# A decoder layer on one Trainium2 core: rows of x in own places and a chunk ahead, gated rows' transposes a chunk later, four chunks of seven products in the second gate/up unit

## The chip, the cores and the metric

The kernel runs on one core of one Trainium2 chip. The metric is the device time of one execution in microseconds. Three executions of the kernel before gave 2029.17, 2032.1 and 2034.15 us, median 2032.1 us. One more execution was recorded by the hardware profiler; it took 2031.15 us.

## What is computed

One layer of a decoder on 256 tokens of width 2048, in float32:

```python
h = h + 0.5 * swiglu(rmsnorm(h, g_ffn1[l]), w1_gate[l], w1_up[l], w1_down[l])
z = rmsnorm(h, g_mix[l]) @ w_in[l]
y = jnp.concatenate([rmsnorm(y_a, g_a_out[l]), rmsnorm(y_b, g_b_out[l])], axis=-1)
h = h + y @ w_out[l]
h = h + cross_attention(rmsnorm(h, g_x[l]), rmsnorm(mem, g_mem[l]),
                        w_xq[l], w_xkv[l], w_xo[l])
h = h + 0.5 * swiglu(rmsnorm(h, g_ffn2[l]), w2_gate[l], w2_up[l], w2_down[l])
```

The change concerns the two feed-forward blocks, `swiglu(x) = (silu(x @ w_gate) * (x @ w_up)) @ w_down`, with 2048 inputs and 5632 inner columns.

## The kernel before, in words

**Exactness.** TensorE is fed float32r values. Every float32 operand is split into a high part and a rest (`split`, L146: ScalarE casts the high part, VectorE subtracts it), and a product is made of three matmuls: high times high, rest times high, high times rest (`passes`, L424, and `run`, L444, whose matmul is L447).

**Units and chunks.** A feed-forward block begins with eleven gate/up units (`gu_unit`, L725). Unit `c` takes 512 columns of the gate and 512 of the up weights through all 2048 inputs, in eight chunks of 256 inputs. A chunk's weights are one load of 1 MB on SyncE's DMA queue (SP) into one of three `raw` places (`load`, L347), and are split into `wh` (ScalarE) and `wl` (VectorE), two places each. A chunk multiplies 2 by 2 blocks of tokens and inputs with 2 by 2 blocks of weights. Kind N does so by eight block products, 24 matmuls. Kind C also by eight, but arranged so that its results can be summed with those of kind S. Kind S does it by seven products (Strassen's way), 21 matmuls; for these VectorE also makes sums of weights (`t`, L356 to L360), which are split too (`th` on ScalarE, `tl` on VectorE). Of the other operand, the normed tokens, an S or C chunk needs differences of blocks as well as the blocks (`fill_sums`, L272, for the first block's `n1`). A pair of 128-row tiles of x, transposed, is called pair `i`; chunk `i` multiplies it. Pair 0 is of kind D, which holds the differences for both C and S.

**Which kinds.** `FEWER = "CCSCSCSC"` has three S chunks, `MORE = "SCSCSCSC"` four. In `gu_unit` (L737) units 2 to 9 take `MORE`, the others `FEWER`; in the first block, unit 0 is all N (`plain_gu_unit`, L753), since its tokens are still being split while it runs.

**Order of work.** TensorE's order is the program's. On the other engines a scheduler sets the order, at build time; it is fixed when the kernel runs. `push` (L513) first loads and splits a chunk's weights, then runs the chunk before it (`turn`, L505). `later` is a list of steps that are put off by a number of chunks. When a unit ends, `late` (L728) gathers its results (`seven_late`, L601), gates them (`gated`, L713), and `rows_done` (L692) puts off, for each of the two blocks of 128 tokens, `turned_rows` (L150): ScalarE copies the gated rows into two 16-bit halves (L153), and SP starts a DMA transpose of them (L156). The first block of tokens is put off by 0, the second by 1. SP issues in order: a weight load behind a transpose isn't issued before it.

**First unit of the first block.** `prep1` (L920) loads pair `i+1` of x while chunk `i` is prepared, into a place of a pool of six (`s2`), and, at 3 to 5, loads x itself and squares it for the norm. `first_pairs` (L889) scales pair `i` by the norm's gain, splits it in time for chunk `i`, and puts its differences off by one chunk.

Of the kernel before, what the change touches and what calls it, by code (L numbers as in the profile page):

```python
# [11 lines left out]
AF = mybir.ActivationFunctionType  # L12
ALU = mybir.AluOpType
# [4 lines left out]
TB = 2  # L18
# [15 lines left out]
def layer_kernel(  # L34
# [22 lines left out]
    nc = tc.nc  # L57
# [13 lines left out]
    def nm(s):  # L71
        uid[0] += 1
        return f"{s}_{uid[0]}"

    def m4(s):
        return mid.tile([P, 1024], F32, tag="m4", name=nm(s))

    def s2(s):
        return tmp.tile([P, 512], F32, tag="s2", name=nm(s))
# [4 lines left out]
    sm = const.tile([P, N_SMALL], F32, name="sm")  # L84
# [61 lines left out]
    def split(hi, lo, src):  # L146
        nc.scalar.copy(hi, src)  # L147
        nc.vector.tensor_tensor(lo, src, hi.bitcast(F32), ALU.subtract)  # L148

    def turned_rows(s, dst, src):  # L150

        w = s2(s + "w").bitcast(U16)
        nc.scalar.copy(  # L153
            w.rearrange("p (h c) -> p h c", h=2), src.bitcast(U16).rearrange("p (c h) -> p h c", h=2)
        )
        nc.sync.dma_start_transpose(dst, w)  # L156

    def tile_turned(s):
        return m4(s).bitcast(U16).rearrange("p (b c t) -> p b c t", b=TB, c=8)
# [109 lines left out]
            fill(s, p, raw)  # L269
        return p  # L270

    def fill_sums(s, p, raw):  # L272

        f = s2(s + "f").rearrange("p (k t) -> p k t", k=4)
        if p.kind == "C":
            f = f[:, :2, :]
            nc.vector.tensor_tensor(f, raw[:, 0::2, :], raw[:, 1::2, :], ALU.subtract)
        else:
            nc.vector.tensor_tensor(
                f[:, 0:2, :], raw[:, 1:2, :].to_broadcast([P, 2, P]), raw[:, 0::3, :], ALU.subtract  # L280
            )
            nc.vector.tensor_tensor(f[:, 2, :], raw[:, 0, :], f[:, 1, :], ALU.subtract)
            nc.vector.tensor_tensor(f[:, 3, :], raw[:, 2, :], f[:, 2, :], ALU.subtract)
        split(p.sums[0], p.sums[1], f)
        if p.kind == "D":
            d = s2(s + "d")[:, :256].rearrange("p (k t) -> p k t", k=2)
            nc.vector.tensor_tensor(d, raw[:, 0::2, :], raw[:, 1::2, :], ALU.subtract)
            split(p.more[0], p.more[1], d)

    def rows_of(srcT, i):  # L290
        return srcT[i * T:(i + 1) * T, :].rearrange("(k p) t -> p k t", p=P)
# [179 lines left out]
    piece = [0]  # L471
# [23 lines left out]
    later = []  # L495
# [17 lines left out]
    def push(u, i, w, p, post=None, pieces=None, beside=None, before=None, ending=None):  # L513
        if before is not None and i:
            before(i)
        b = load(u.s, w, u.kinds[i], pieces, lambda n: before(i, n) if i == 0 else None)
        if beside is not None:
            beside(i)

        def run():  # L520
            first, last = [f("S") if "S" in u.kinds else -1 for f in (u.kinds.find, u.kinds.rfind)]
            if u.late and all(name in u.left for name in u.late):
                held[0] = first <= i <= last

                ends[0] = now[0] + 2 if u.clear and i == first - 1 else None
            held[0] = held[0] or i in u.alone
            tight[0] = u.sparse and first <= i <= last
            if ending is None:
                u.multiply(u.kinds[i], p(), b, i in (0, len(u.kinds) - 1))
            elif not u.kept:  # L530
                u.kept.append((p(), b))
            else:
                u.multiply_two(u.kept[0], (p(), b), ending)
            held[0] = False
            ends[0] = None

        turn(run, post)
# [42 lines left out]
    FEWER, MORE = "CCSCSCSC", "SCSCSCSC"  # L580
# [20 lines left out]
    def seven_late(u, got, dst):  # L601

        p1, v, z = got["p1"], got["v"], got["z"]
        nc.vector.tensor_tensor(dst(0, 0), u["P2"], p1, ALU.add)
        nc.vector.tensor_tensor(dst(1, 1), u["Q5"], z, ALU.add)
        nc.vector.tensor_tensor(v, u["Q5"], v, ALU.add)  # L606
        nc.vector.tensor_tensor(dst(0, 1), u["Q3"], v, ALU.add)
        nc.vector.tensor_tensor(dst(1, 0), u["Q4"], z, ALU.subtract)
# [79 lines left out]
    def ffn(s, get, rs, wgu, wd, on_block, first=None, on_token_block=None):  # L688
# [3 lines left out]
        def rows_done(c, rows_):  # L692
            t = tile_turned(s + "a")

            def turned(tb):
                turned_rows(s, t[:, tb], rows_[tb])
                for q in range(2):
                    acts[2 * c + q] = t

            for tb in range(TB):  # L700
                later.append((tb, lambda tb=tb: turned(tb)))

        def joined(i):
            turned_ = by_block(have(acts, i))
# [8 lines left out]
        def gated(up, sg, r, tb):  # L713
            nc.scalar.activation(sg[1], sg[0], AF.Silu, scale=r[:, tb:tb + 1])
            nc.vector.scalar_tensor_tensor(
                out=sg[1], in0=up, scalar=r[:, tb:tb + 1], in1=sg[1], op0=ALU.mult, op1=ALU.mult
            )

        def inner(i):
            if pairs[i] is None:  # L720
                raw = joined(i)
                pairs[i] = Pair(s + "a", KINDS_D[i])
                fill(s + "a", pairs[i], raw)

        def gu_unit(c):  # L725
            got = {}

            def late(u):  # L728
                r = rs()
                c22 = s2(s + "u")  # L730
                at = {(0, 0): got["p1"], (1, 1): c22, (0, 1): got["v"], (1, 0): got["z"]}
                seven_late(u, got, lambda tb, j: at[tb, j])
                gated(at[0, 1], (at[0, 0], at[0, 0]), r, 0)
                gated(c22, (at[1, 0], at[1, 0]), r, 1)
                rows_done(c, (at[0, 0], at[1, 0]))

            kinds = MORE if 2 <= c <= 9 else FEWER  # L737
            order = range(8)
            if c == (first is not None):
                order = ORDER[first is None]  # L740
            u = Unit(s + "g", "".join(kinds[j] for j in order))
            for i in range(8):
                push(
                    u, i, wgu[order[i], c], lambda j=order[i]: get(j),
                    lambda i=i: (
                        i == u.kinds.rindex("S") and seven_early(u, got), i == 7 and late(u)
                    ),
                    beside=lambda i: (
                        rs() if (c, i) == (0, 5) else inner(i - 5) if c == 10 and i >= 5 else None
                    ),  # L750
                )
# [30 lines left out]
        for n, idx in enumerate(turns):  # L782
            half = n % 2
            kinds = "".join(KINDS_D[i] for i in idx)
# [98 lines left out]
    n1 = [None] * 8  # L883
    parts1 = tiny.tile([P, TB, NG], F32, tag="parts", name=nm("parts"))
    rs1 = []

    ahead = []

    def first_pairs(i, piece=None):  # L889

        if not piece:
            n1[i] = Pair("n1", KINDS[i], "N")
            if piece is not None:
                ahead.append(s2("n1r").rearrange("p (k t) -> p k t", k=2))
        if piece is None:
            for k in range(2):
                scaled_row(i, k)
            split(*[t.rearrange("p k t -> p (k t)") for t in n1[i].base],
                  ahead[0].rearrange("p k t -> p (k t)"))
        elif piece in (0, 2):  # L900
            k = piece // 2
            nc.sync.dma_start(ahead[0][:, k, :], xT[k * P:(k + 1) * P, :])
            row_loaded(n1[i], ahead[0], i, k, G_FFN1)
        if piece in (None, 2):
            raw = ahead.pop(0)

            def sums():
                if piece is not None:
                    for k in range(2):
                        scaled_row(i, k, raw)  # L910
                fill_sums("n1", n1[i], raw.rearrange("p k (b t) -> p (k b) t", b=TB))

            later.append((1, sums))

    def scaled_row(i, k, raw=None):
        o = (raw or ahead[0])[:, k, :]
        c = G_FFN1 + 2 * i + k
        nc.scalar.activation(o, o, AF.Copy, scale=sm[:, c:c + 1])

    def prep1(i):  # L920
        if i < 7:
            ahead.append(s2("n1r").rearrange("p (k t) -> p k t", k=2))
            nc.sync.dma_start(ahead[-1], rows_of(xT, i + 1))
        for j in {3:(0,1),4:(2,3)}.get(i, ()):
            blocks_of_x(j)
        for j in {4:(0,1),5:(2,3)}.get(i, ()):
            for tb in range(TB):
                square_into(parts1[:, tb, j:j + 1], h[:, tb, j * 512:(j + 1) * 512], 512)
        if i == 5:
            rs1.append(rstd_of(parts1, NG, D))  # L930

    def blocks_of_x(j0):
# [8 lines left out]
        first=(first_pairs, prep1),  # L941
# [573 lines left out]
```

## Time and profile before

| what | value |
|---|---|
| median of three executions | 2032.1 us |
| profiled execution, its own time | 2031.15 us |
| span of its profile, first to last instruction | 2029.3 us |
| TensorE busy | 2012.1 us, 99% |
| VectorE busy | 1854.5 us, 91% |
| ScalarE busy | 1306.9 us, 64% |
| granted TensorE clock, mean | 0.999 |
| HBM read | 398.52 MB, 197 GB/s over the span |

In the rows of the profile PE is TensorE's matmuls and PEld its weight loads, DVE is VectorE, ACT is ScalarE, POOL is GpSimd, SPq is SyncE's queue that issues DMAs. A row of the timeline has start in us, duration in us, engine, line, operation, out<-in, how often, and in brackets the idle time before it and what ended that. A row of the table of waits has the waiting engine and what it waited for, then us in total, times, and the longest. A row of a stretch has its bounds, its length, and for each engine busy us and (x) its number of instructions. In the view of one tile, an operation's duration is min/median/max in ns, and the time from issue to landing in us. A tile's name begins with the block's part: `f1g` is the first block's gate/up, `f1d` its down projection, `f2` the second block; `f1gQ`, `f1gP`, `f1gR` are accumulators, `f1gw` the loaded weights.

### The profile page before, as it was taken

To read this page: it belongs to the slowest core of one execution; us is meant where nothing else is said; L and a number is where in the kernel's file an instruction comes from. 1 tells how busy PE (TensorE), PEld (TensorE's weight loads), DVE (VectorE), ACT (ScalarE), POOL (GpSimd) and SP (SyncE) were. 2 spreads that over 40 slices of the span, in tenths; PEclk is the share of its full clock that TensorE was granted. 3 is DMA by queue.
4 is the path that set the end of the run, shared out by engine and by line. 5 is a ranking of instruction groups with operands and counts; after the bars stand their busy time and mean duration, and the time that the engine had idled before them with its cause. 6 is when DMAs were issued, how large, how long until landed. Compare 5 with 4: busy or idle time off the path is not lost.

```text
span 2029.3 us, 24175 instructions
## 1 busy us (share of the span) xinstructions
PE 2012.1 (99%) x9168; PEld 1664.4 (82%) x9168; DVE 1854.5 (91%) x1988; ACT 1306.9 (64%) x1440; POOL 34.0 (2%) x57
## 2 busy tenths in 40 slices
PE   9999999999999999999999999999999999999998
PEld 7888878888888888888888888888888888888886
DVE  6999999999999978989878977899999999999998
ACT  7656656567665766655557666675656665676664
POOL 0000000000000010100000000000000000000000
PEclk9999999999999999999999999999999999999999
DMA  8566666666555565545665544556666656665563
GB/s 312 201 240 206 214 218 200 228 216 220 203 192 206 184 240 191 192 166 175 210 218 188 205 149 148 181 186 228 198 235 213 219 204 238 209 218 206 187 227 125
DMA packets 115332, 415.82 MB, mean 205 GB/s; under 512 B 61824, under 2 KB 63888, under 8 KB 68112
## 3 DMA queue, kind: packets, MB, share of 16 engines
q1 hardware_dynamic: 112768, 407.14, 57.9%
q0 software_dynamic: 2016, 6.30, 1.0%
q8 instruction: 72, 1.18, 0.2%
q10 hardware_dynamic: 432, 0.84, 0.1%
q14 instruction: 44, 0.36, 0.1%
HBM read 398.52 MB, written 2.10 MB: 197 GB/s over the span
## 4 chain that ended last, share of the span: by engine, by line
PE 84%; DVE 7%; issue 4%; ACT 2%; DMA 2%; SPq 0%; POOL 0%; DVEq 0%; POOLq 0%; ACTq 0%
PE f2gQ L447 13%; PE f1gQ L447 11%; PE f2dQ L447 6%; PE f1dQ L447 6%; PE f2gP L447 4%; PE f1gP L447 4%; PE xqQ L447 3%; PE f2dP L447 3%; PE f1dP L447 3%; PE woQ L447 2%; PE xoQ L447 2%; PE f2dR L447 2%; PE f1dR L447 2%; PE mv0Q L447 2%; PE vQ L447 2%
## 5 line engine op out<-in xcount | busy, mean ns | idle before, releaser
L148 DVE TENSOR_TENSOR f1gwl<-f1gw,f1gwh 128x1536 fp32r<-128x1536 f32 (+2 forms) x94 | 181.6, 1934 | 23.2 <-ACT f1gwh L147 23.2
L147 ACT CAST f1gwh<-f1gw 128x1536 fp32r<-128x1536 f32 (+2 forms) x94 | 152.3, 1626 | 62.7 <-PE f1gQ L447 41.6
L147 ACT CAST f2gwh<-f2gw 128x1536 fp32r<-128x1536 f32 (+1 forms) x88 | 150.5, 1711 | 61.4 <-PE f2gQ L447 41.4
L148 DVE TENSOR_TENSOR f2gwl<-f2gw,f2gwh 128x1536 fp32r<-128x1536 f32 (+1 forms) x88 | 179.0, 2035 | 9.1 <-ACT f2gwh L147 9.1
L147 ACT CAST f2gth<-f2gt 128x1024 fp32r<-128x1024 f32 x82 | 85.8, 1050 | 67.5 <-DVE f2gt L360 37.8
L447 PE MATMUL f1gQ<-f1gwh,n1fh 128*128 128x512 f32 x318 | 124.3, 391 | 1.6 <-DVE f1gv L606 1.6
L447 PE MATMUL f2gQ<-f2gwh,n4fh 128*128 128x512 f32 x317 | 124.2, 392 | 0.3
L447 PE MATMUL f1gQ<-f1gwh,n1fl 128*128 128x512 f32 x318 | 123.7, 389 | 0.0
L447 PE MATMUL f2gQ<-f2gwh,n4fl 128*128 128x512 f32 x317 | 123.4, 389 | 0.0
L147 ACT CAST f1gth<-f1gt 128x1024 fp32r<-128x1024 f32 x76 | 79.4, 1051 | 63.7 <-DVE f1gt L360 38.2
L147 ACT CAST f2dwh<-f2dw 128x2048 fp32r<-128x2048 f32 (+1 forms) x44 | 77.4, 1760 | 47.4 <-PE f2dQ L447 42.6
L147 ACT CAST f1dwh<-f1dw 128x2048 fp32r<-128x2048 f32 (+1 forms) x44 | 77.3, 1757 | 40.9 <-PE f1dQ L447 37.2
L148 DVE TENSOR_TENSOR f1dwl<-f1dw,f1dwh 128x2048 fp32r<-128x2048 f32 (+1 forms) x44 | 92.1, 2092 | 11.5 <-ACT f1dwh L147 11.4
L148 DVE TENSOR_TENSOR f2dwl<-f2dw,f2dwh 128x2048 fp32r<-128x2048 f32 (+1 forms) x44 | 92.1, 2093 | 11.2 <-ACT f2dwh L147 11.1
L148 DVE TENSOR_TENSOR f2gtl<-f2gt,f2gth 128x1024 fp32r<-128x1024 f32 x82 | 99.6, 1217 | 1.0
L447 PE MATMUL f1gQ<-f1gwl,n1fh 128*128 128x512 f32 x318 | 97.5, 389 | 0.0
L447 PE MATMUL f2gQ<-f2gwl,n4fh 128*128 128x512 f32 x317 | 96.7, 389 | 0.0
L148 DVE TENSOR_TENSOR f1gtl<-f1gt,f1gth 128x1024 fp32r<-128x1024 f32 x76 | 92.2, 1218 | 1.0
L447 PEld LDWEIGHTS f1gQ<-f1gwh,n1fh 128*128 128x128 f32 x318 | 59.7, 188 | 15.8 <-DVE f1gv L606 3.5
L447 PEld LDWEIGHTS f2gQ<-f2gwh,n4fh 128*128 128x128 f32 x317 | 59.5, 188 | 14.8 <-DVE f2gv L606 2.6
L447 PE MATMUL f1gP<-f1gwh,n1fl 128*128 128x512 f32 x176 | 68.9, 392 | 1.3 <-DVE n1fl L148 1.3
L447 PEld LDWEIGHTS f1gQ<-f1gwl,n1fh 128*128 128x128 f32 x318 | 59.7, 188 | 12.6 <-DVE f1gwl L148 0.2
(790 smaller groups left out, 6017.5 us busy)
## 6 DMA issues: line engine op xcount, KB each, us to landing
f2gw<-in_w_gu SPq DMA_DIRECT2D x88, 1024.0 KB, 4.9
f1gw<-in_w_gu SPq DMA_DIRECT2D x86, 1024.0 KB, 5.2
f1dw<-in_w_down SPq DMA_DIRECT2D x44, 1024.0 KB, 4.8
f2dw<-in_w_down SPq DMA_DIRECT2D x44, 1024.0 KB, 4.8
wow<-in_w_out SPq DMA_DIRECT2D x16, 1024.0 KB, 4.9
xqw<-in_w_xq SPq DMA_DIRECT2D x16, 1024.0 KB, 4.8
xow<-in_w_xo SPq DMA_DIRECT2D x16, 1024.0 KB, 4.8
qw<-in_w_in SPq DMA_DIRECT2D x8, 1024.0 KB, 4.8
```

The source lines that it names most:

```text
L147: nc.scalar.copy(hi, src)
L148: nc.vector.tensor_tensor(lo, src, hi.bitcast(F32), ALU.subtract)
L447: nc.tensor.matmul(self.banks[name], x, y, start=name not in self.begun, stop=self.left[name] == 0)
```

## The change

Three things, in the first feed-forward block for the first two, in both blocks for the third:

- Pair `i` of x is loaded into a place of its own (halves of four tiles of the larger pool `m4`), loaded a chunk earlier for pairs 4 to 7, and split a chunk earlier: at chunk 3 pairs 3 and 4 are split, at chunks 4 to 6 pairs 5 to 7. Differences of pairs are put off by two chunks, those of pairs 2 and 3 by one. The loads and squares of x come a chunk later. For pairs 0 to 2 some of these instructions keep the program's order.
- In the first block, unit 1 takes `MORE` instead of `FEWER`: its chunk 0 is S instead of C.
- Transposes of gated rows are put off by 1 and 2 chunks instead of 0 and 1.

```diff
-                later.append((tb, lambda tb=tb: turned(tb)))
+                later.append((tb + 1, lambda tb=tb: turned(tb)))
...
-            kinds = MORE if 2 <= c <= 9 else FEWER
+            kinds = MORE if (2 if first is None else 1) <= c <= 9 else FEWER
...
+    def raw_x(i):
+
+        if i % 2 == 0:
+            raws.append(m4("n1r").rearrange("p (i k t) -> p i k t", i=2, k=2))
+        return raws[-1][:, i % 2]
 
     def first_pairs(i, piece=None):
+
+        if piece is not None or i < 3:
+            first_pair(i, piece)
+        elif i == 3:
+            first_pair(3)
+            first_pair(4)
+        elif i < 7:
+            first_pair(i + 1)
...
+                placed = tc.keep_in_program_order if i < 3 else lambda ins: ins
                 if piece is not None:
                     for k in range(2):
-                        scaled_row(i, k, raw)
-                fill_sums("n1", n1[i], raw.rearrange("p k (b t) -> p (k b) t", b=TB))
-
-            later.append((1, sums))
+                        placed(scaled_row(i, k, raw))
+                fill_sums("n1", n1[i], raw.rearrange("p k (b t) -> p (k b) t", b=TB), placed)
+
+            later.append((1 if i in (2, 3) else 2, sums))
...
     def prep1(i):
-        if i < 7:
-            ahead.append(s2("n1r").rearrange("p (k t) -> p k t", k=2))
-            nc.sync.dma_start(ahead[-1], rows_of(xT, i + 1))
-        for j in {3:(0,1),4:(2,3)}.get(i, ()):
+        for q in {0: (1,), 1: (2,), 2: (3, 4), 3: (5,), 4: (6,), 5: (7,)}.get(i, ()):
+            ahead.append(raw_x(q))
+            nc.sync.dma_start(ahead[-1], rows_of(xT, q))
+        for j in {4:(0,1),5:(2,3)}.get(i, ()):
             blocks_of_x(j)
-        for j in {4:(0,1),5:(2,3)}.get(i, ()):
+        for j in {5:(0,1),6:(2,3)}.get(i, ()):
             for tb in range(TB):
                 square_into(parts1[:, tb, j:j + 1], h[:, tb, j * 512:(j + 1) * 512], 512)
-        if i == 5:
+        if i == 6:
             rs1.append(rstd_of(parts1, NG, D))
```

**SP, at the end of the first block's unit 1** (`f1gw` are loads of weights for the following chunks, `f1a` the transposed gated rows of unit 1). Before:

```order
L377 DMA f1gw_936<-in_w_gu 128x2048
L156 DMA_TRANSPOSE f1a_853<-f1w_854 128x8x128
L156 DMA_TRANSPOSE f1a_853<-f1w_891 128x8x128
L354 DMA f1gw_963<-in_w_gu 128x2048
L377 DMA f1gw_1005<-in_w_gu 128x2048
```

Changed:

```order
L377 DMA f1gw_941<-in_w_gu 128x2048
L156 DMA_TRANSPOSE f1a_858<-f1w_893 128x8x128
L354 DMA f1gw_968<-in_w_gu 128x2048
L156 DMA_TRANSPOSE f1a_858<-f1w_938 128x8x128
L377 DMA f1gw_1010<-in_w_gu 128x2048
```

The first transpose stands where it stood; the second has moved behind one load of weights. It is so after units 0 to 8 of the first block and 1 to 8 of the second. After unit 10 of both, where one load stood between the two transposes, both now stand behind it; after the other units nothing moves on SP.

**ACT, in the first unit, from the cast of chunk 2's weights on.** Before, `f1gw_222` and `f1gw_264` are the weights of chunks 2 and 3, and `n1r_228` and `n1r_270` the rows of pairs 3 and 4:

```order
L147 CAST f1gwh_223<-f1gw_222 128x2048
L918 ACTIVATE n1r_228<-n1r_228,sm 128x256 x2
L147 CAST n1fh_258<-n1r_228 128x512
L147 CAST f1gwh_265<-f1gw_264 128x2048
L147 CAST n1fh_216<-n1f_298 128x512
```

Changed, `f1gw_209` and `f1gw_268` are those weights, and `n1r_128`, `n1r_171`, `n1r_216` hold pairs 0 and 1, 2 and 3, 4 and 5:

```order
L147 CAST f1gwh_210<-f1gw_209 128x2048
L936 ACTIVATE n1r_128<-n1r_128,sm 128x256 x2
L936 ACTIVATE n1r_171<-n1r_171,sm 128x256 x2
L936 ACTIVATE n1r_216<-n1r_216,sm 128x256 x2
L147 CAST f1gwh_269<-f1gw_268 128x2048
L147 CAST n1fh_124<-n1f_244 128x512
L147 CAST n1fh_254<-n1r_171 128x512
L147 CAST n1fh_260<-n1r_216 128x512
```

Six scalings of rows stand between the two casts of weights, and the casts of pairs 3 (`n1fh_254`) and 4 stand behind them.

**DVE, in the same place.** Before, `n1fl_259` is the rest of pair 3:

```order
L148 TENSOR_TENSOR f1gwl_224<-f1gw_222,f1gwh_223 128x2048
L148 TENSOR_TENSOR n1fl_259<-n1r_228,n1fh_258 128x512
L279 TENSOR_TENSOR n1f_298<-n1r_172 128x256
L282 TENSOR_TENSOR n1f_298<-n1r_172,n1f_298 128x128
L283 TENSOR_TENSOR n1f_298<-n1r_172,n1f_298 128x128
L148 TENSOR_TENSOR f1gwl_266<-f1gw_264,f1gwh_265 128x2048
```

Changed, `n1fl_255` is the rest of pair 3:

```order
L148 TENSOR_TENSOR f1gwl_211<-f1gw_209,f1gwh_210 128x2048
L279 TENSOR_TENSOR n1f_244<-n1r_128 128x256
L282 TENSOR_TENSOR n1f_244<-n1r_128,n1f_244 128x128
L283 TENSOR_TENSOR n1f_244<-n1r_128,n1f_244 128x128
L148 TENSOR_TENSOR f1gwl_270<-f1gw_268,f1gwh_269 128x2048
L148 TENSOR_TENSOR n1fl_125<-n1f_244,n1fh_124 128x512
L287 TENSOR_TENSOR n1d_250<-n1r_128 128x256
L148 TENSOR_TENSOR n1fl_255<-n1r_171,n1fh_254 128x512
```

The rest of pair 3 stood right behind the rest of chunk 2's weights; it now stands behind the rest of chunk 3's weights and the differences of pair 0.

More of the change, by code (lines that the diff above doesn't have):

```diff
@@ L270, in pair_from_rows, with fill_sums @@
         return p
-    def fill_sums(s, p, raw):
+    def fill_sums(s, p, raw, placed):
         f = s2(s + "f").rearrange("p (k t) -> p k t", k=4)
@@ L276, in fill_sums @@
             f = f[:, :2, :]
-            nc.vector.tensor_tensor(f, raw[:, 0::2, :], raw[:, 1::2, :], ALU.subtract)
+            placed(nc.vector.tensor_tensor(f, raw[:, 0::2, :], raw[:, 1::2, :], ALU.subtract))
         else:
-            nc.vector.tensor_tensor(
+            placed(nc.vector.tensor_tensor(
                 f[:, 0:2, :], raw[:, 1:2, :].to_broadcast([P, 2, P]), raw[:, 0::3, :], ALU.subtract
-            )
+            ))
             nc.vector.tensor_tensor(f[:, 2, :], raw[:, 0, :], f[:, 1, :], ALU.subtract)
@@ L286, in fill_sums @@
             d = s2(s + "d")[:, :256].rearrange("p (k t) -> p k t", k=2)
-            nc.vector.tensor_tensor(d, raw[:, 0::2, :], raw[:, 1::2, :], ALU.subtract)
+            placed(nc.vector.tensor_tensor(d, raw[:, 0::2, :], raw[:, 1::2, :], ALU.subtract))
             split(p.more[0], p.more[1], d)
@@ L887, in layer_kernel, with first_pair @@
     ahead = []
-    def first_pairs(i, piece=None):
+    raws = []
+    def raw_x(i):
+        if i % 2 == 0:
+            raws.append(m4("n1r").rearrange("p (i k t) -> p i k t", i=2, k=2))
+        return raws[-1][:, i % 2]
+    def first_pairs(i, piece=None):
+        if piece is not None or i < 3:
[5 more added lines that the diff above has]
+            first_pair(i + 1)
+    def first_pair(i, piece=None):
         if not piece:
@@ L893, in first_pairs @@
             if piece is not None:
-                ahead.append(s2("n1r").rearrange("p (k t) -> p k t", k=2))
+                ahead.append(raw_x(0))
         if piece is None:
@@ L917, in scaled_row @@
         c = G_FFN1 + 2 * i + k
-        nc.scalar.activation(o, o, AF.Copy, scale=sm[:, c:c + 1])
+        return nc.scalar.activation(o, o, AF.Copy, scale=sm[:, c:c + 1])
     def prep1(i):
-        if i < 7:
-            ahead.append(s2("n1r").rearrange("p (k t) -> p k t", k=2))
-            nc.sync.dma_start(ahead[-1], rows_of(xT, i + 1))
-        for j in {3:(0,1),4:(2,3)}.get(i, ()):
+        for q in {0: (1,), 1: (2,), 2: (3, 4), 3: (5,), 4: (6,), 5: (7,)}.get(i, ()):
+            ahead.append(raw_x(q))
+            nc.sync.dma_start(ahead[-1], rows_of(xT, q))
+        for j in {4:(0,1),5:(2,3)}.get(i, ()):
             blocks_of_x(j)
-        for j in {4:(0,1),5:(2,3)}.get(i, ()):
+        for j in {5:(0,1),6:(2,3)}.get(i, ()):
             for tb in range(TB):
                 square_into(parts1[:, tb, j:j + 1], h[:, tb, j * 512:(j + 1) * 512], 512)
-        if i == 5:
+        if i == 6:
             rs1.append(rstd_of(parts1, NG, D))
```

## The prediction

> **What bounds the kernel now.** First the page's busy times and its chain of waits:
>
> ```profile
> PE 2012.1 (99%) x9168; PEld 1664.4 (82%) x9168; DVE 1854.5 (91%) x1988; ACT 1306.9 (64%) x1440; POOL 34.0 (2%) x57
> PE 84%; DVE 7%; issue 4%; ACT 2%; DMA 2%; SPq 0%; POOL 0%; DVEq 0%; POOLq 0%; ACTq 0%
> ```
>
> TensorE is at work for 99% of the span, and the chain runs through it for 84%. So a gain is either fewer matmuls or a removed stall of TensorE. The table of waits says what there is to remove:
>
> ```profile
> PE f1gQ L447 <- DVE f1gv L606: 1.6, 4, 0.9
> PE f1gP L447 <- DVE n1fl L148: 1.3, 1, 1.3
> PE f1gP L447 <- DVE f1gwl L148: 1.2, 1, 1.2
> PEld f1gQ L447 <- DVE f1gv L606: 3.5, 5, 1.3
> PEld f2gQ L447 <- DVE f2gv L606: 2.6, 6, 0.6
> ```
>
> Nearly all of it lies in the gate/up units, and VectorE ends it. Two places matter: the first unit (`n1fl`, the rest of a pair) and the ends of units (L606 reads the accumulator that the next unit needs). By unit, in stretches:
>
> ```profile
> 53.20:94.70 41.50, 41.50 (x185) 34.38 (x184) 37.21 (x34) 24.13 (x22) 0.00 (x0) 1.00 0.66 225
> 94.70:135.50 40.80, 40.80 (x182) 33.80 (x181) 39.53 (x37) 25.19 (x22) 0.00 (x0) 1.00 0.62 219
> ```
>
> These are units 1 and 2 of the first block; behind the length stand the busy times of PE, PEld and DVE. A unit of four S chunks takes TensorE 40.80 us, one of three 41.50. VectorE has 39.5 us of work in the 40.80, so it can hardly make up lost time. It loses time, in the first block's units 4 to 9, at the same place of each; the timeline of VectorE:
>
> ```profile
> 190.90 1.76 DVE L148 TENSOR_TENSOR f1gwl<-f1gw,f1gwh 128x1536 fp32r<-128x1536 f32 x1 [0.72 <-ACT f1gwh L147]
> 234.44 1.76 DVE L148 TENSOR_TENSOR f1gwl<-f1gw,f1gwh 128x1536 fp32r<-128x1536 f32 x1 [3.09 <-ACT f1gwh L147]
> 275.89 1.76 DVE L148 TENSOR_TENSOR f1gwl<-f1gw,f1gwh 128x1536 fp32r<-128x1536 f32 x1 [1.00 <-ACT f1gwh L147]
> 317.28 1.76 DVE L148 TENSOR_TENSOR f1gwl<-f1gw,f1gwh 128x1536 fp32r<-128x1536 f32 x1 [0.94 <-ACT f1gwh L147]
> 399.53 1.76 DVE L148 TENSOR_TENSOR f1gwl<-f1gw,f1gwh 128x1536 fp32r<-128x1536 f32 x1 [0.47 <-ACT f1gwh L147]
> ```
>
> From 275.89 to 317.28 are 41.39 us: without the 0.94 of idle VectorE would take 40.45, less than TensorE. ScalarE, for which it waits, itself waits for a load that SP issued behind two transposes:
>
> ```profile
> 222.25 2.61 SPq L156 DMA_TRANSPOSE f1a<-f1w  x2
> 224.95 0.52 SPq L354 DMA_DIRECT2D f1gw<-in_w_gu  x1
> 221.72 2.28 DVE L148 TENSOR_TENSOR f1gwl<-f1gw,f1gwh 128x2048 fp32r<-128x2048 f32 x1
> 232.93 1.48 ACT L147 CAST f1gwh<-f1gw 128x1536 fp32r<-128x1536 f32 x1 [4.44 <-DMA f1gw<-in_w_gu]
> 268.50 5.78 DMA f1gw<-in_w_gu
> f2gw<-in_w_gu SPq DMA_DIRECT2D x88, 1024.0 KB, 4.9
> f1a<-f1w SPq DMA_TRANSPOSE x22, 3.2
> ```
>
> The load's place is free at 224.0 (VectorE's row at 221.72); it is issued at 224.95 and used at 232.93, 8.0 us on. A unit later it takes 5.78 (the chain of waits), while the median load takes 4.9 (the DMA view, from issue to landing).
>
> **The change, part by part.**
>
> *Four S chunks in unit 1.* Three matmuls fewer; their duration is start to start, 2.72 us for 12:
>
> ```profile
> 49.05 2.72 PE f1gQ L447 x12
> ```
>
> So 3 x 0.227 = **-0.7 us**. VectorE gets more: for the C chunk's rest (2.29) it now makes the sums (1.23 + 0.69 + 0.69), the smaller rest (1.76) and two rests of sums (1.22 each):
>
> ```profile
> 63.15 1.23 DVE L356 TENSOR_TENSOR f1gt<-f1gw 128x1024 f32<-128x1024 f32 x1 [1.34 <-DMA f1gw<-in_w_gu]
> 64.41 0.69 DVE L359 TENSOR_TENSOR f1gt<-f1gt,f1gw 128x512 f32<-128x512 f32 x1
> L148 DVE TENSOR_TENSOR f1gtl<-f1gt,f1gth 128x1024 fp32r<-128x1024 f32 x76 | 92.2, 1218 | 1.0
> ```
>
> That is 6.8 for 2.3, +4.5 us, and 37.21 + 4.5 = 41.7 us of work in 40.80. Its cover is the idle time of VectorE in the first unit's last chunks and in unit 1 (41.50 - 37.21 = 4.3 us), and a lead: L606 of unit 1 ends at 94.80, and TensorE needs the bank at 95.81.
>
> ```profile
> 94.12 0.68 DVE L606 TENSOR_TENSOR f1gv<-f1gQ,f1gv 128x512 f32<-128x512 f32 x1
> 95.81 0.39 PE L447 MATMUL f1gQ<-f1gwh,n1fh 128*128 128x512 f32 x1
> ```
>
> 0.9 of excess against 1.0 of lead: I take nothing. If the cover fails, it costs what is missing, at most the 4.5. A gain is excluded: VectorE only gets work.
>
> *The first unit.* What there is to gain:
>
> ```profile
> 17.20 0.61 PE L447 MATMUL f1gQ<-f1gwl,n1fh 128*128 128x512 f32 x2
> 18.60 0.50 PE L447 MATMUL f1gP<-f1gwh,n1fh 128*128 128x512 f32 x1 [0.78 <-ACT f1gwh L147]
> 42.16 0.50 PE L447 MATMUL f1gP<-f1gwh,n1fl 128*128 128x512 f32 x1 [1.26 <-DVE n1fl L148]
> ```
>
> Start to start the first stall is 18.60 - 17.20 - 0.45 = 0.95, the second 1.26 plus some 0.2 of refilled pipeline; with the refill both cost 2.6 us. Both should go: pair 6 is split a chunk earlier, and the cast of chunk 2's weights stands behind fewer casts. But a third appears, by the order of ScalarE and VectorE shown above. The rows for it:
>
> ```profile
> L377 SPq DMA_DIRECT2D f1gw<-in_w_gu x1: 883/883/883, 7.7 to 7.7; - x1
> DMA to landing us min/median/max: 7.8/7.8/7.8
> 16.65 1.90 ACT L147 CAST f1gwh<-f1gw 128x2048 fp32r<-128x2048 f32 x1
> 18.45 0.91 ACT L918 ACTIVATE n1r<-n1r,sm 128x256 f32<-128x256 f32 x2
> 18.58 2.29 DVE L148 TENSOR_TENSOR f1gwl<-f1gw,f1gwh 128x2048 fp32r<-128x2048 f32 x1 [0.99 <-ACT f1gwh L147]
> 20.78 0.69 DVE L148 TENSOR_TENSOR n1fl<-n1r,n1fh 128x512 fp32r<-128x512 f32 x1
> ```
>
> Chunk 2's weights land at 7.7 + 7.8 = 15.5; the cast begins at once, not at 16.65, and is done at 17.4, in time for the end of chunk 1 at 17.66 (17.20 + 2 x 0.227). Start to start it takes 1.80 (16.65 to 18.45). Then, from 17.3, ScalarE scales six rows, two of which take 0.91 with a little overlap, 2.6 in all, to 19.9, and casts chunk 3's weights to 21.8. VectorE's rest of these takes 2.2 start to start (18.58 to 20.78), to 24.0; then come a rest of 512 columns, a difference of 256 and the rest of pair 3, by the 0.69 at 20.78 some 0.6 + 0.35 + 0.69: 25.6. TensorE ends chunk 2 at 17.66 + 24 x 0.227 = 23.1 and needs that rest one matmul later, at 23.3. The new stall is 2.3 us. So the first unit gives 2.6 - 2.3 = **-0.3 us**. If chunk 3's casts come sooner than the rows say it is up to -2.6; if a later chunk's split is also late, +1.
>
> *The loads' places.* Halves of tiles from a pool of twelve instead of a pool of six: loads of x no longer wait for a place. x itself and its squares come a chunk later; their result is first used by the gate at the end of the unit, two chunks on. I cost both at nothing; what hides them is those two chunks, 48 matmuls or 10.9 us. If the norm were late, the gate and with it the bank for unit 1 would wait, by at most the 5.4 us of the chunk that they move.
>
> *The transposes.* Nothing is removed: 22 in each block still run. Per unit one of the two moves behind a load, and ScalarE's copy for it behind a cast of sums. The load ahead is issued when its place is free, 0.9 us sooner, and has one transpose ahead of it instead of two. Its landing is sooner by at least 0.9 and at most by a transpose's 3.2; I take 1.9, twice the usual idle of 0.94. VectorE then takes 40.45 per unit, TensorE 40.80, and the stalls at L606 go. Their size in the first block: 399.53 - 190.90 = 208.6 us for five units, against 5 x 40.80 = 204.0: 4.6 us late, of which the stalls of the table, 1.6 + 1.2 idle, are the least that reached TensorE. I take **-3.8**, between them, nearer to the upper because each stall also refills the pipeline. In the second block:
>
> ```profile
> 1436.02 1.76 DVE L148 TENSOR_TENSOR f2gwl<-f2gw,f2gwh 128x1536 fp32r<-128x1536 f32 x1 [1.07 <-ACT f2gwh L147]
> 1723.48 1.76 DVE L148 TENSOR_TENSOR f2gwl<-f2gw,f2gwh 128x1536 fp32r<-128x1536 f32 x1 [0.33 <-ACT f2gwh L147]
> ```
>
> 287.5 us for seven units against 285.6: 1.9 at most; I take **-1.5**. Late next is VectorE itself, by 0.35 us of spare time a unit. The waiting instruction is the second transpose, on SP: behind it stands the next load, which the rows have at 226.90 and cast at 239.86:
>
> ```profile
> 226.90 0.33 SPq L377 DMA_DIRECT2D f1gw<-in_w_gu  x1
> 239.86 3.29 ACT L147 CAST f1gwh<-f1gw 128x2048 fp32r<-128x2048 f32 x2
> ```
>
> It was behind the transpose before as well; against 13 us of distance one transpose's 3.2 is covered. After unit 10 both transposes stand behind a load; their rows are read five chunks later, so nothing.
>
> The Trainium skill speaks against this term: by "DMA: Bandwidth & Descriptors", section Queues, rings and completion order, the DMAs of one issuing engine share one ring on each DMA engine, which takes descriptors in ring order. The trace's 8.0 us behind two transposes against 4.9 agrees. By that rule the second load gains nothing, since the bytes in front of it are the same; with half of the term lost the sum would be -3.7 instead of -6.3.
>
> **Sum.** -0.7 - 0.3 - 3.8 - 1.5 = -6.3 us from the profiled execution's 2031.15 (its span of 2029.3 and 1.85 around it): 2024.9. That execution was 0.95 below the median, so the median becomes 2032.1 - 6.3 = **2025.8 us**. A measurement of this kernel tells some 0.3%, 6.1 us, from no change; the sum lies on that edge.
>
> **The rivals.**
>
> *Handed on (0.22).* The second load, now between two transposes' queues, takes over the wait. For it: a load behind transposes was late (8.0 and 5.78 against 4.9), and one still is. Against it: the 13 us until that load is cast. Half of -5.3 stays: 2032.1 - 0.7 - 0.3 - 2.6 = 2028.5. Ring order, named above, is this case.
>
> *A better start (0.16).* The new stall of chunk 3 isn't there, and all stalls at L606 go: -0.7 - 2.6 - 4.6 - 1.9 = -9.8, 2022.3. Against it: the order of the two engines, which is fixed.
>
> *Nothing (0.07).* VectorE is what is late, not the loads; with one more S chunk it stays so. Only the matmuls are saved: 2031.4.
>
> *Slower (0.05).* From unit 1 on the load behind the second transpose is late as at 234.44, 3.09 us in each of the nine units. VectorE's 40.45 becomes 43.5, TensorE loses 2.7 in each, 24.7 us, less the 4.6 that it loses now and the 0.7: +19, 2051. It decides where idle time per unit passes 0.35 + (4.6 + 0.7 + 6.1) / 9 = 1.6 us. For it: the one case of 3.09. Against it: the other rows stay at 1.0 or less.
>
> **How the numbers follow.** The forecast has 0.50, with some 2 us to either side for its terms. It is split by the edge of 6.1 us: 0.30 beyond, 0.20 within. With the better start 0.16 and 0.01 of the handed-on case that makes faster 0.47; slower is 0.05; within 0.3% the rest, 0.48. The range goes from 2021.5, the better start with its measurement's spread, to 2031.0, short of nothing gained; it leaves out most of the last two cases and a tail below.
>
> **What would show it.** Right: the matmuls of `f1gQ` fewer by three; no idle time of 0.8 at chunk 2 and of 1.3 at chunk 6, but one of some 2 us before `n1fl` at 23 to 26; VectorE's idle time before `f1gwl` in units 4 to 9 below 0.3; waits of PEld for L606 near nothing; unit to unit 40.8 us. Wrong: those idles unchanged with a sooner load (then VectorE's work decides), idle time elsewhere in the same units (handed on), or waits of PE for `f1gtl` in unit 1 (the fourth S chunk has no cover).

## The result, and the profile after

The median of seven runs of the kernel after is 2024.76 us (2024.18 to 2027.58); the kernel before, in seven runs, has 2031.3 us (2029.17 to 2034.15). The ratio is 0.9967, with a 95% interval of 0.9957 to 0.9977: 6.5 us, a third of a per cent; the interval lies to both sides of the 0.3% named in the prediction, so that the change is faster is settled, that it is so by over 0.3% is not. The profiled execution went from 2031.15 to 2024.46 us, its span from 2029.3 to 2022.8.

The page's busy times and its chain of waits, of the kernel after:

```profile
PE 2007.2 (99%) x9165; PEld 1665.3 (82%) x9165; DVE 1859.3 (92%) x1993; ACT 1305.5 (65%) x1442; POOL 34.0 (2%) x57
PE 73%; DVE 3%; issue 1%; ACT 1%; POOL 0%; POOLq 0%; DVEq 0%
```

Three matmuls fewer, and VectorE 4.8 us busier. The shares of the chain add up to 78% only: followed back, it breaks off at 460 us and leaves out nearly all of the first block's gate/up units, so they can't be set against the 84% and 7% of before. The table of waits (us in all, times, the longest) shows what is left of the waits for `n1fl` and L606:

```profile
PE f1gP L447 <- DVE n1fl L148: 2.1, 1, 2.1
PEld f1gP L447 <- DVE n1fl L148: 3.1, 2, 2.5
PE f1dQ L447 <- DVE f1gv L606: 0.2, 1, 0.2
```

L606 no longer holds up a gate/up unit (the row that is left is the hand-over to the down projection). The one stall of TensorE in the first unit, once it runs, is the new one. VectorE's timeline at the places where it is idle in units 5, 6, 7 and 9:

```profile
226.78 2.29 DVE L148 TENSOR_TENSOR f1gwl<-f1gw,f1gwh 128x2048 fp32r<-128x2048 f32 x1 [0.32 <-ACT f1gwh L147]
267.58 2.29 DVE L148 TENSOR_TENSOR f1gwl<-f1gw,f1gwh 128x2048 fp32r<-128x2048 f32 x1 [0.32 <-ACT f1gwh L147]
308.38 2.29 DVE L148 TENSOR_TENSOR f1gwl<-f1gw,f1gwh 128x2048 fp32r<-128x2048 f32 x1 [0.31 <-ACT f1gwh L147]
...
389.98 2.29 DVE L148 TENSOR_TENSOR f1gwl<-f1gw,f1gwh 128x2048 fp32r<-128x2048 f32 x1 [0.31 <-ACT f1gwh L147]
```

From 226.78 to 389.98 are 163.20 us for four units, 40.80 each to the hundredth: TensorE's own time of a unit sets the pace. The idle time now stands ahead of another operation, the rest of a whole chunk (2048 columns, where it was the 1536 of an S chunk). ScalarE's timeline says what its casts wait for, and SP's how the transposes and loads stand:

```profile
265.63 1.92 ACT L147 CAST f1gwh<-f1gw 128x2048 fp32r<-128x2048 f32 x1 [1.87 <-PE f1gQ L447]
269.26 1.49 ACT L147 CAST f1gwh<-f1gw 128x1536 fp32r<-128x1536 f32 x1 [0.77 <-PE f1gQ L447]
```

```profile
261.90 1.24 SPq L156 DMA_TRANSPOSE f1a<-f1w  x1
263.29 0.48 SPq L354 DMA_DIRECT2D f1gw<-in_w_gu  x1
263.81 1.24 SPq L156 DMA_TRANSPOSE f1a<-f1w  x1
266.16 0.33 SPq L377 DMA_DIRECT2D f1gw<-in_w_gu  x1
```

The cast at 269.26 is the counterpart, one unit on, of the one that waited 4.44 us for its load before (232.93 in the prediction's rows). It now waits for TensorE to give up the place that it writes (PE f1gQ), though not by much: its load, issued at 263.29, landed at 269.04, 5.8 us on. The load is issued 1.4 us after the first transpose, where it was 2.7 before (222.25 to 224.95 in the prediction's rows).

Where the time came from is read from the starts of TensorE's first matmul of each name: the first unit (first `f1gP` to the last `f1gR`), the ten other gate/up units of the first block (to the first `f1d`), what lies between the blocks, the second block's gate/up units (first `f2g` to first `f2d`), and the rest. All times are in us, of one profile each; the rows behind the second are experiments told below.

| kernel | first unit | units 1 to 10 | between | second block | rest |
|---|---|---|---|---|---|
| before | 46.91 | 414.28 | 868.50 | 455.61 | 238.14 |
| after | 46.77 | 408.91 | 869.10 | 453.33 | 238.65 |
| transposes only | 46.41 | 411.18 | 868.56 | 453.32 | 238.27 |
| transposes back | 46.74 | 411.75 | 868.55 | 460.71 | 238.16 |
| fourth chunk only | 46.47 | 413.91 | 868.33 | 458.09 | 238.16 |
| rows only | 47.13 | 414.39 | 868.65 | 455.68 | 238.15 |
| sums later | 46.74 | 408.91 | 868.61 | 454.16 | 238.76 |
| sums last, three chunks | 44.99 | 411.14 | 868.69 | 453.29 | 238.74 |
| from ScalarE's queue | 47.28 | 425.76 | 875.37 | 465.79 | 238.16 |
| plain copies, before | 47.10 | 410.05 | 868.23 | 453.29 | 238.21 |
| plain copies, after | 48.44 | 408.91 | 868.17 | 453.33 | 238.67 |

From before to after: -0.1, -5.4, +0.6, -2.3, +0.5. Both blocks have a floor, the time without a stall: 408.91 comes out three times to the hundredth (with three S chunks in unit 1 it would be 0.7 more, 409.6), 453.3 five times. Where the transposes stand in their new places, both blocks run at TensorE's own speed, but for single late loads (below).

### The profile page after: what moved, and what is told of

Read it like the earlier page. It is cut to its first block, busy times and chain, and to the rows that moved or that the text cites. A ratio compares the mean times of both kernels' runs of the same rounds, so it can differ in the third digit from the quotient of the medians.

```text
span 2022.8 us, 24182 instructions
## 1 busy us (share of the span) xinstructions
PE 2007.2 (99%) x9165; PEld 1665.3 (82%) x9165; DVE 1859.3 (92%) x1993; ACT 1305.5 (65%) x1442; POOL 34.0 (2%) x57
## 4 chain that ended last, share of the span: by engine, by line
PE 73%; DVE 3%; issue 1%; ACT 1%; POOL 0%; POOLq 0%; DVEq 0%
PE f2gQ L447 16%; PE f2dQ L447 6%; PE f1dQ L447 6%; PE f2gP L447 6%; PE xqQ L447 3%; PE f2dP L447 3%; PE f1dP L447 3%; PE woQ L447 2%; PE xoQ L447 2%; PE f2dR L447 2%; PE f1dR L447 2%; PE mv0Q L447 2%; PE vQ L447 2%; PE mv1Q L447 2%; PE mk1Q L447 2%; PE mk0Q L447 2%
## 5 line engine op out<-in xcount | busy, mean ns | idle before, releaser
L447 PEld LDWEIGHTS f2gQ<-f2gwh,n4fl 128*128 128x128 f32 x317 | 59.5, 188 | 12.3
L447 PEld LDWEIGHTS f2gQ<-f2gwl,n4fh 128*128 128x128 f32 x317 | 59.4, 188 | 12.3
```

The costliest lines, as they stand in the source:

```text
L447: nc.tensor.matmul(self.banks[name], x, y, start=name not in self.begun, stop=self.left[name] == 0)
```

## The experiments

Each was timed in five rounds beside the kernel before, whose medians over its runs were 2030.8 to 2031.4 us.

**Transposes only.** The kernel before with one edit:

```
-                later.append((tb, lambda tb=tb: turned(tb)))
+                later.append((tb + 1, lambda tb=tb: turned(tb)))
```

> The kernel before, with the one edit that each unit's two transposes run a chunk later. Theory (the loads behind the transposes made VectorE late, and TensorE with it): the stalls at L606 go in both blocks, 4.7 us in the first and 2.3 in the second, so the time falls by 6 to 7 us against the kernel before, VectorE's idle time before f1gwl falls to some 0.3 us, and the units are 40.8 us apart. Rival handed on (the second load takes over half of the wait): 2.6 us less, idle times of some 1 us elsewhere in the units. Rival nothing (VectorE itself is late): within 1 us.

2024.76 us, ratio 0.9967 (0.9954 to 0.9979): the whole gain of the change, by one line of it. The second block is at 453.32; the first is 1.6 us above its floor of 409.6, by a load that came late (on VectorE, L606 follows that of the unit before by 43.0 us there, and by 40.6 and 40.4 after it):

```profile
226.92 2.29 DVE L148 TENSOR_TENSOR f1gwl<-f1gw,f1gwh 128x2048 fp32r<-128x2048 f32 x1 [0.32 <-ACT f1gwh L147]
288.95 1.22 DVE L356 TENSOR_TENSOR f1gt<-f1gw 128x1024 f32<-128x1024 f32 x1 [2.38 <-DMA f1gw<-in_w_gu]
```

That load was issued 11 us after the unit's transposes had landed, and took 7.5 us instead of 4.9. So late loads of this size also come without a transpose; this is returned to below.

**Transposes back.** The reverse edit in the kernel after.

> The kernel after, with the transposes put back to where they stood before; rows of x and the fourth S chunk stay. Theory (transposes carry the gain): the idle time before f1gwl is back at about 1 us in units 4 to 9, the stalls at L606 are back, and the time is 6 to 7 us above the kernel after, within 1 us of the kernel before. Rival (rows and fourth S chunk carry it): within 2 us of the kernel after. Rival (the fourth S chunk's 4.5 us of VectorE work have no cover without the later transposes): 2 to 4 us slower than the kernel before.

2031.01 us, ratio 0.9999 (0.9990 to 1.0008): the gain is gone, and the rest of the change neither gains nor loses. The waits are back, in this profile in the second block above all (460.71 in the table):

```profile
PEld f2gQ L447 <- DVE f2gv L606: 5.1, 6, 1.3
```

The idle times in the first block are 0.4 to 1.0 us, near the "about 1 us" expected. How much the old places cost differs from one execution to the next: the second block took 455.61, 455.68, 458.09 and 460.71 us in the four profiles that have them, although VectorE, ScalarE and SP have the same order there in all four.

**Fourth chunk only.** The kernel before with `MORE if (2 if first is None else 1) <= c <= 9` for the kinds.

> The kernel before, with a fourth chunk of seven products in unit 1 and nothing else. Theory (VectorE's idle time in unit 1 and the lead at its end cover the 4.5 us of work): three matmuls fewer, 0.7 us less. Rival (no cover while the transposes delay the loads, since VectorE then has no spare time in the later units to make it up): up to 3.8 us more, as stalls at L606 of units 1 to 3.

2031.05 us, ratio 0.9996 (0.9987 to 1.0005): 0.7 less is inside the interval, 3.8 more is not. At the ends of units 1 to 3 TensorE comes to its bank 0.4 to 0.8 us late, which the kernel before doesn't, so some of the 4.5 us of VectorE's work is seen. TensorE's timeline at the end of unit 1, here and with the transposes back (the kernel after with that one edit):

```profile
95.80 0.50 PE L447 MATMUL f1gQ<-f1gwh,n1fh 128*128 128x512 f32 x1 [0.28 <-DVE f1gv L606]
```

```profile
94.64 0.39 PE L447 MATMUL f1gP<-f1gwl,n1fh 128*128 128x512 f32 x1
94.87 0.39 PE L447 MATMUL f1gQ<-f1gwh,n1fh 128*128 128x512 f32 x1
```

With the transposes back but the rows of x in their new places, unit 1 ends without a stall and takes 40.80 us, as in the kernel after; here it takes 41.47, as much as with three S chunks before (41.48). So, by one profile each, it is the rows of x that give the fourth S chunk its cover, not the later transposes.

**Rows only.** The kernel after with the transposes back and three S chunks in unit 1.

> The kernel after, with the transposes put back and three S chunks in unit 1: of the change only the rows of x in own places, split a chunk ahead, are left. Theory (the stall at chunk 3 takes the place of the two that go): a stall of some 2 us at chunk 3, the start of unit 1 within 0.3 us of the kernel before, the time within 0.5 us of the kernel before. Rival (the rows start the whole block earlier, and gain by themselves): 2 us or more less than the kernel before.

2032.49 us, ratio 1.0004 (0.9994 to 1.0013). The stall at chunk 3 is there without the other two edits, on TensorE's timeline, so it belongs to the rows:

```profile
26.03 0.50 PE L447 MATMUL f1gP<-f1gwh,n1fl 128*128 128x512 f32 x1 [2.08 <-DVE n1fl L148]
```

**Sums later.** The kernel after, with the sums of pair 0 one chunk later:

```
-            later.append((1 if i in (2, 3) else 2, sums))
+            later.append((3 if i == 0 else 1 if i in (2, 3) else 2, sums))
```

> The kernel after, with the sums of pair 0 made a chunk later, which by the order puts the split of pairs 3 and 4 ahead of chunk 3's cast on ScalarE and ahead of its rest on VectorE. Theory (the new stall of 2.3 us at 25.86 is n1fl of pair 3 behind chunk 3's rest): that stall goes, nothing else changes, 2.3 us less than the kernel after, 9 us less than the kernel before. Rival (chunk 3's weights are what is late): a stall of 1 to 2 us moves to f1gwh or f1gwl of chunk 3, and the time is within 1 us of the kernel after.

2024.7 us, ratio 0.9968 (0.9956 to 0.9981): nothing gained over the kernel after, and for a reason that neither theory had. The stall at chunk 3 did go, but two others came, at chunks 5 and 7:

```profile
35.80 0.50 PE L447 MATMUL f1gP<-f1gwh,n1fl 128*128 128x512 f32 x1 [1.36 <-DVE n1fl L148]
47.66 0.50 PE L447 MATMUL f1gP<-f1gwl,n1fh 128*128 128x512 f32 x1 [0.46 <-DVE f1gwl L148]
```

The first unit takes 46.74 us against 46.77. The sums that were put off stood in front of the next pair's rest instead.

**Sums last.** All sums of x are put off further, and the last chunk's weights go ahead of them:

```
+            later.append(({0: 4, 1: 4, 2: 4, 3: 3}.get(i, 2), sums))
...
+                with tc.high_priority():
+                    split(wh, wl, raw)
```

> The kernel after, with the sums of the pairs of x put off by up to two chunks more and the last chunk's weights ahead of them, so that by the order each rest that the first unit needs itself stands ahead of the sums that only unit 1 needs. Theory (VectorE's work in the first 55 us is more than TensorE leaves room for, and putting off only moves the stall): no stall in the first unit, but stalls of 1 to 3 us in unit 1 at f1gwl or f1gtl of its first S chunk, the time within 1 us of the kernel after. Rival (only the order is at fault): no stall in either, 2.3 us less than the kernel after.

2027.23 us, ratio 0.9980 (0.9972 to 0.9989), 2.5 us more than the kernel after. The first unit's stall is gone, and unit 1 has three instead, 3.0 us together (it takes 45.00 us instead of 40.80), as the theory had it; only "within 1 us of the kernel after" was too little:

```profile
52.40 0.50 PE L451 MATMUL f1gP<-f1gwl,n1fh 128*128 128x512 f32 x1 [0.63 <-DVE f1gwl L148]
55.40 0.50 PE L451 MATMUL f1gQ<-f1gtl,n1fh 128*128 128x512 f32 x1 [0.66 <-DVE f1gtl L148]
59.07 0.50 PE L451 MATMUL f1gQ<-f1gtl,n1fh 128*128 128x512 f32 x1 [1.72 <-DVE f1gtl L148]
```

**Sums last, three chunks.** The same with three S chunks in unit 1, whose first two chunks then need no sums of weights.

> The kernel with the sums of x last, as in the run before this, but with three chunks of seven products in unit 1 as in the kernel before, so that its first two chunks need no sums of weights. Theory (VectorE's work around the start of unit 1 is what decides there): the stalls of 3.5 us at 52 to 59 go, three matmuls come back (0.7 us), and no stall of 2.3 us stands in the first unit: 1 to 2 us less than the kernel after, some 8 us less than the kernel before. Rival (the stall moves on, to the S chunks of unit 1): the time of the kernel after or more.

2023.36 us (2022.11 to 2024.29), ratio 0.9961 (0.9948 to 0.9973). This has the lowest median of the study: by the ratio 7.9 us below the kernel before, and by the medians 1.4 below the kernel after. The second step is not settled, since the intervals overlap; the profile supports it, with 44.99 us for the first unit against 46.77 and no stall over 0.3 us in it or in unit 1. The profiled execution would be some 1.5 us shorter without a late load at 287.38 (411.14 against the floor of 409.6).

**One more VectorE operation.** The kernel after, with the sum of L605 made twice in each gate/up unit but the first, the first time ahead of the others:

```
+                nc.vector.tensor_tensor(c22, u["Q5"], got["z"], ALU.add)
                 seven_late(u, got, lambda tb, j: at[tb, j])
```

> The kernel after, with one more VectorE operation in each gate/up unit but the first: the sum of L605 is made twice, 0.68 us a unit, ahead of L606. It changes no result. Theory (VectorE has 0.31 us of spare time a unit): its idle time before f1gwl is used up, 0.37 us a unit is missing, and stalls at L606 return; with 10 and 11 units 3 to 8 us more than the kernel after. Rival (with the transposes behind a load VectorE has room, since the loads alone set its pace): within 1 us of the kernel after.

2043.67 us, ratio 1.0060 (1.0047 to 1.0072): 19 us more than the kernel after, where 3 to 8 was expected. Most units are 41.75 to 41.80 us long instead of 40.80. The edit did more than it was to do: the scheduler also put the sums of the next unit's weights (L356) ahead of L605 and L606, and the two transposes next to each other. So the same was run with a smaller operation, in the same order.

**The same, 128 columns.** `nc.vector.tensor_tensor(c22[:, :128], u["Q5"][:, :128], got["z"][:, :128], ALU.add)`.

> As the run with one more VectorE operation of 0.68 us in each gate/up unit, but the operation has 128 columns and takes some 0.29 us; the order of every queue is otherwise the one of that run, both transposes together between two loads. Theory (only VectorE's spare time of 0.31 us a unit counts): 0.29 fits, no stalls at L606, within 2 us of the kernel after. Rival (that order makes the load behind the two transposes late again, which showed as 0.7 us of idle time before f1gwl): the idle time stays at 0.7, stalls at L606 stay, and only the 0.39 us a unit between the two operations are saved, 8 us of the 19: some 10 us more than the kernel after.

2033.69 us, ratio 1.0016 (1.0007 to 1.0025), 9 us above the kernel after: the number that the rival named. But its reason is not what the profile shows. VectorE's timeline at the turn from unit 3 to 4, here and in the kernel after:

```profile
175.84 0.28 DVE L732 TENSOR_TENSOR f1u<-f1gQ,f1gz 128x128 f32<-128x128 f32 x1
176.04 1.22 DVE L356 TENSOR_TENSOR f1gt<-f1gw 128x1024 f32<-128x1024 f32 x1
177.17 0.68 DVE L605 TENSOR_TENSOR f1u<-f1gQ,f1gz 128x512 f32<-128x512 f32 x1
177.77 0.68 DVE L606 TENSOR_TENSOR f1gv<-f1gQ,f1gv 128x512 f32<-128x512 f32 x1
...
187.85 2.29 DVE L148 TENSOR_TENSOR f1gwl<-f1gw,f1gwh 128x2048 fp32r<-128x2048 f32 x1 [0.67 <-ACT f1gwh L147]
```

```profile
174.52 0.68 DVE L605 TENSOR_TENSOR f1u<-f1gQ,f1gz 128x512 f32<-128x512 f32 x1
175.12 0.68 DVE L606 TENSOR_TENSOR f1gv<-f1gQ,f1gv 128x512 f32<-128x512 f32 x1
176.31 0.68 DVE L607 TENSOR_TENSOR f1gv<-f1gQ,f1gv 128x512 f32<-128x512 f32 x1
176.91 1.22 DVE L356 TENSOR_TENSOR f1gt<-f1gw 128x1024 f32<-128x1024 f32 x1
```

In the kernel after L606 ends at 175.8 and TensorE starts on its bank at 176.76: about 1.0 us of lead. Here 0.20 + 1.13 us (start to start) stand in front of L605, 0.3 more than the lead; TensorE starts 0.42 late, refills, and the unit is 41.4 us long. With the larger operation it is 0.61 + 1.13, 0.7 more than the lead: 0.82 late, 41.8. VectorE meanwhile is idle for 0.7 us a unit at 187.85, behind a cast whose load had landed at 177.10. So neither theory holds: by these rows it is not VectorE's spare time in the unit that decides, and not a late load, but what stands ahead of L606 at the turn. No run puts the operation at another place of the unit, which would test this.

**Transposes from ScalarE's queue.** The kernel before, with `nc.scalar.dma_start_transpose(dst, w)` for `nc.sync`. (The eight transposes of `mkw`, which the same helper issues, move too.)

> The kernel before, with the transposes issued from ScalarE's queue and not from SP's; they stand where they stood, right behind their copies. Theory (the load is late because it stands in the queue behind two transposes, of which SP's own issuing takes 0.9 us): the load lands 4.9 to 5.5 us after its issue, the stalls at L606 go, and the time is 5 to 7 us less than the kernel before. Rival (the transposes and the load share the same engines' time, whatever queue they come from): the load still takes 7 to 8 us, and the time is within 2 us of the kernel before. Rival (issuing costs ScalarE 2.6 us a unit ahead of a cast): new idle time of VectorE before f1gtl, the time at or above the kernel before.

2059.8 us (2044.9 to 2069.5), ratio 1.0132 (1.0099 to 1.0165): 28 us slower, worse than any theory had. ScalarE's timeline, the DMA view of 224 to 250 us and that of the whole span (median from issue to landing last):

```profile
225.82 2.65 ACTq L156 DMA_TRANSPOSE f1a<-f1w  x2
238.97 1.48 ACT L147 CAST f1gwh<-f1gw 128x1536 fp32r<-128x1536 f32 x1 [6.64 <-DMA f1gw<-in_w_gu]
```

```profile
f1gw<-in_w_gu SPq DMA_DIRECT2D x4, 1024.0 KB, 12.6
f1a<-f1w ACTq DMA_TRANSPOSE x2, 9.0
```

```profile
f1a<-f1w ACTq DMA_TRANSPOSE x22, 5.5
f2a<-f2w ACTq DMA_TRANSPOSE x22, 6.3
```

In one queue a transpose took 3.2 us and the loads behind two of them 5.8 to 8.4; side by side from two queues both take longer, up to 14.8 us a load. Of the 28 us some 7 lie between the blocks, where `mkw` is. The second rival had the cause, not the size; the third shows too, but only in 1.4 us of new waits of TensorE for `f1gth` and `f2gth`. The Trainium skill says what the second rival says, in "DMA: Bandwidth & Descriptors", section Issuing engines are not separate DMA queues: whichever engine starts them, DMAs run on the same 16 engines and interleave, and a second queue saves only issuing time. These rows agree, and add that a transpose and 1 MB loads side by side took longer here than one behind the other.

**Plain copies, before and after.** In both kernels each transpose is made a copy of the same bytes at the same place, and the turning is left out: `nc.sync.dma_start(dst, w.rearrange("p (c t) -> p c t", c=8))`. The order of every engine stays. (The eight of `mkw` are copies too, 52 in all.)

> The kernel before, with each of its 44 transposes made a plain copy of the same 256 KB, in the same place of SP's queue; the order of every engine stays. The turning of the gated rows is left out, so the second half of the feed-forward multiplies unturned rows. Theory (what delays the loads is how long a transpose keeps the 16 DMA engines, not that something stands ahead of them in the queue): the load behind lands within 6 us, the stalls at L606 go, and the time is 6 to 8 us less than the kernel before, as with the transposes moved. Rival (order in the queue: two transfers and SP's waits for their copies stand ahead): 3 us less at most, VectorE's idle time before f1gwl stays above 0.7.

> The kernel after, with the same edit: plain copies for the transposes, in the places that they have there; the turning is left out. Theory (moving the transposes has taken away nearly all that they cost): within 2 us of the kernel after, units 40.80 us apart. Rival (half of their cost was handed on to the second load, in the second block above all): 2.5 us or more less than the kernel after.

Before with copies: 2024.53 us, ratio 0.9965 (0.9952 to 0.9977). After with copies: 2025.74 us, ratio 0.9971 (0.9960 to 0.9982), within 1 us of the kernel after. The DMA view of the first and its SP timeline:

```profile
f1a<-f1w SPq DMA_DIRECT2D x22, 256.0 KB, 2.3
f2a<-f2w SPq DMA_DIRECT2D x22, 256.0 KB, 2.3
```

```profile
262.63 1.42 SPq L156 DMA_DIRECT2D f1a<-f1w  x2
264.18 0.50 SPq L354 DMA_DIRECT2D f1gw<-in_w_gu  x1
```

Two copies still stand ahead of the load in the same queue; it landed at 269.10, 4.9 us after its issue, and of the stalls at L606 one of 0.5 us is left. It is the transposing that delays, 3.2 us against 2.3 each and 2.6 us of SP's issuing against 1.4 for both, not that something stands in front; which of these two counts for more isn't told apart. Nor is it ScalarE's order, which moving the transposes also changes: here it stays. And moving the transposes has taken away all that they cost here: with copies nothing more is gained.

## Why the prediction was right

**The bound.** TensorE behind VectorE at the ends of units, VectorE behind a load: shown, by taking the delay away in two ways (moved, or made copies), which give the same 6.5 to 7 us.

**Three matmuls, -0.7.** They are gone, and unit 1 takes 40.80 us in the profile instead of 41.48. In the times of the whole it can't be told from nothing: the version with neither them nor the rows (transposes only) has the same median. The cover was better than worked out: 0.9 of the 1.0 us of lead should have been used up, and 0.8 was left (L606 ends at 94.33, TensorE comes to the bank at 95.16). It hangs on the rows, which the prediction didn't say: without them unit 1 gained nothing (fourth chunk only).

**The first unit, -0.3.** The new stall stands where it was put and is 2.1 us of idle time, and makes TensorE 2.3 us late from start to start; its chain came as forecast:

```profile
20.04 1.89 ACT L147 CAST f1gwh<-f1gw 128x2048 fp32r<-128x2048 f32 x1
21.84 0.61 ACT L147 CAST n1fh<-n1f 128x512 fp32r<-128x512 f32 x1
```

```profile
21.97 2.29 DVE L148 TENSOR_TENSOR f1gwl<-f1gw,f1gwh 128x2048 fp32r<-128x2048 f32 x1 [0.92 <-ACT f1gwh L147]
...
25.11 1.29 DVE L148 TENSOR_TENSOR n1fl<-n1r,n1fh 128x512 fp32r<-128x512 f32 x2
```

The prediction had the cast at 19.9, VectorE's rest to 24.0 and the pair's to 25.6; the rows have 20.04, 24.2 and 25.8. The unit gained 0.1. "The order of the two engines" was said to be what holds back the better start; that was half of it. With pair 0's sums a chunk later the stall moved to chunks 5 and 7, and with all sums late to unit 1. It goes only when VectorE also gets less to do there.

**The transposes, -3.8 and -1.5.** The mechanism was right, the sizes were low: at the floors the first block gave 5.4 less the 0.7 of the matmuls, 4.7, and the second 2.3. The row that gave 4.6 as the most for five units was nearer to the truth than the value taken between it and 2.8. For the second block the upper end of 1.9 counted seven units; and how late the old places made a block differs between executions, up to 7.4 us there. One part of the 4.6 is not surely the transposes' own: the idle time of 3.09 was one late load, and such loads come in the new order too (2.38, 2.32 us). Two more differences weren't foreseen. The 0.6 between the blocks is within what the profiles differ by there (868.17 to 869.10 without the ScalarE queue's). The 0.5 behind them isn't: the table has 238.65 to 238.76 wherever rows and transposes have both moved and 238.27 or less elsewhere, and 0.4 of it lies behind the last matmul; its cause is open. With these the profiled execution gained 6.7 us against the 6.3 of the sum. That it came so near is in part luck: the transposes gave 1.7 more than taken, and these two took 1.1 back.

**Handed on.** Didn't happen. The second load (issued at 266.16 in the rows after) landed at 272.56, and its cast at 276.34 waited for nothing. The bytes in front, by which the rival counted, are not what delayed the first load either: behind two plain copies of the same size it was in time.

**Slower, by VectorE.** The price of 2.7 us a unit needed idle times of 1.6; they were 0.3. But the statement behind it, that VectorE's 0.35 us to spare in a unit decide, is what fell: 0.28 us more, with an order that it changed, cost 9 us while VectorE idled more than before. By the rows the unit has a second limit, the 1.0 us between L606 and the next use of its bank.

## What to carry over

Where one engine is 99% busy, look for the operation that gives back what it needs next, and count the work ahead of that operation at that moment: by the rows here that lead decides, not the other engine's spare time over the unit. A slow transfer in front of an urgent load can cost more than its bytes, as the transposes did here beside copies of the same size; let the load go first, and test before giving the slow one a queue of its own, which cost 28 us here. When a stall is removed by reordering, look for it at the next places of the same engine before counting the gain; here it took less work as well to make it go.

## What was not expected of the hardware

TensorE's granted clock fell to half for 3.4 us after the stall at chunk 3, in two of the six profiles that have this stall. Stretches of 1, 3 and 1 us behind that stall (the granted clock stands ahead of the DMA share), of the kernel with plain copies after, and of the kernel after:

```profile
26.00:27.00 1.00, 1.00 (x5) 0.82 (x5) 1.00 (x4) 1.00 (x4) 0.00 (x0) 0.99 1.03 425
27.00:30.00 3.00, 3.00 (x8) 2.31 (x8) 3.00 (x5) 1.14 (x4) 0.00 (x0) 0.50 1.01 370
30.00:31.00 1.00, 1.00 (x5) 0.78 (x5) 0.97 (x4) 0.62 (x2) 0.00 (x0) 0.81 1.10 410
```

```profile
27.00:30.00 3.00, 3.00 (x15) 2.46 (x14) 3.00 (x5) 1.20 (x4) 0.00 (x0) 1.00 1.01 371
```

Eight matmuls in 3 us instead of fifteen: some 1.7 us lost, the 48.44 of the table. The other profile with the loss is that of one more VectorE operation. The two with the loss idled 2.12 and 2.07 us, the four without 2.10, 2.09, 2.08 and 2.00, so its length alone doesn't decide. The Trainium skill has the gate in "TensorE: Matmul & The Clock Gate", Part 1: a free-running window of some 3.4 us decides, and one idle window halves the clock. The 3.4 us at half speed agree, and a free-running window would explain why the same stall costs sometimes 2.3 and sometimes 4.0 us; but 2.1 us of idle time were enough here.

Single loads of 1 MB took 7.5 us instead of 4.9 without a transpose near, the one at 288.95 above and this one in the fastest version, on VectorE's timeline:

```profile
287.38 1.22 DVE L356 TENSOR_TENSOR f1gt<-f1gw 128x1024 f32<-128x1024 f32 x1 [2.32 <-DMA f1gw<-in_w_gu]
```

Each made one unit some 2 us longer on VectorE, of which the next gave part back. The DMA view of 279 to 290 us has one packet of instructions (0.02 MB) beside two such loads in the fastest version; the same window of the kernel after has one too, and its two loads took 5.0 us, so that alone isn't the cause. What delays them stays open.
